# Retrieval stage of a two-block kernel: one fixed order for TensorE, ScalarE and GpSimd, filling blocks spread over each route, and low halves made by GpSimd in the first two routes

## Chip, cores and metric

One core of one Trainium2 chip runs the whole program in one launch. The metric is the device time of that launch in microseconds (us). The median of three runs of the kernel before is 3214.27 us (3212.13 to 3221.74). A difference of 0.3%, about 9.6 us, is about the least that a measurement of this kernel can tell from no change.

## What is computed

The reference applies two transformer-like blocks to 512 tokens of width 1024. The change lies in the retrieval part of the first block:

```python
def block(xb):                      # 128 tokens at a time
    q = (xb @ w_query).reshape(T, 8, 2, 128)
    s = einsum('thpk,hpnk->thpn', q, sub_keys)         # two score rows of 128 for each head
    top_s, top_i = top_k(s, 16)
    cand_s = top_s[:, :, 0, :, None] + top_s[:, :, 1, None, :]
    cand_i = top_i[:, :, 0, :, None] * 128 + top_i[:, :, 1, None, :]
    best_s, best_pos = top_k(cand_s, 16)               # 16 of 16384 experts for each head
    idx = take_along_axis(cand_i, best_pos)
    gate = softmax(best_s)
    act = gelu(einsum('td,thkd->thk', xb, expert_u[idx]))
    return einsum('thk,thkd->td', gate * act, expert_v[idx])
```

## The kernel before

Four token tiles of 128 are routed. The experts of tile 0 are fetched row by row with indirect DMAs (`sparse`). For tiles 1 to 3 (384 tokens) all 16384 experts are multiplied densely, in 128 blocks of 128 experts, and weighted by a matrix `Wd` that holds the gates where they belong and zero elsewhere.

A **filling block** is one of those 128 blocks of the first product. `usplit` makes it ready: ScalarE casts the loaded `raw` (512 KB) into its high half `whi`, and the engine in `lo_eng[0]` subtracts to get the low half `wlo`. Both halves are 128x1024. `ublock` runs 24 matmuls of 384 columns, 12 before its `yield` and 12 after, and ScalarE's Gelu (`ge`) ends it. Then SP writes the result to `gd` (192 KB). The first `AHEAD = 76` blocks are done in the retrieval stage, to keep TensorE at work while the tiles are routed. `lookahead(nb, ns, nd)` issues 2·nb half blocks, up to nd of the waiting `Wd` writes (256 KB each), and counts ns towards the next gathered row. At the first half of block b it also splits block b+1; there are three pairs of `whi` and `wlo`.

`route(t)` is VectorE's work: sums of candidates (`cs`, `ci`), top 16 for each of eight heads, and for each head a comparison, a product and a sum over 128x800 (`eq`, `ix`). ScalarE's one part in it is the exponential of the softmax. Every `yield` in it lets the caller issue a `lookahead(1, 0)`, one whole block. Its first `yield` stands after the first head's `ix`. For tiles 1 to 3 it ends with three transposes on TensorE, ScalarE's copy `pT`, and VectorE's `nT`.

`scatter(t)` builds `Wd` for a tile, four tokens at a time (32 times): VectorE makes `bo` and three `ao`, ScalarE makes the fourth `ao` (through `ab`), four matmuls write a PSUM tile, and ScalarE copies it to `stg`. The `ao` and `bo` of a step are made one step ahead. After every second step one half block is issued. At the end 32 writes of `stg` to `Wd` are put on the list `pend`.

The order in the program is: route 0 and 1, scatter 1, route 2, scatter 2, route 3, scatter 3, and a tail of whole blocks until 76 are done and `pend` is empty. That makes 19 blocks in the first two routes, 8 in each scatter, 11 in each later route and 11 in the tail. The framework's planner is free to order the instructions of each engine otherwise: among what it takes to be ready, the instruction that was written first goes first. `pin(engines)` takes that freedom away: it chains all instructions of the named engines that were written since `pos[0]`, in the order written. Before the change only the dense stage after the retrieval is pinned. SP's DMA queue runs in the planner's order throughout.

After the tail, the dense stage loads `Wd`, `gd` and `v` for each block (`load`, `mid`) and TensorE runs the second product (`down`).

Of the kernel before, what the change touches and what calls it, by code (L numbers as in the profile page):

```python
# [181 lines left out]
def build(tc, A, out):  # L182
    nc = tc.nc
    V, S, G, PE = nc.vector, nc.scalar, nc.gpsimd, nc.tensor
    with ExitStack() as ctx:
# [52 lines left out]
        def psum(tag="ps"):  # L238
            ps = banks[""].tile([128, T], F32, name=tag, bufs=banks[tag])
            return ps  # L240
# [24 lines left out]
        lo_eng = [G]  # L265
# [42 lines left out]
        def gemm_cm(*a, **k):  # L308
            for _ in gemm_gen(*a, **k):
                pass  # L310
# [148 lines left out]
        with rpool("hg") as hg:  # L459
# [15 lines left out]
            with rpool("hgl") as hl_:  # L475
# [38 lines left out]
                for l in range(9):  # L514
                    m = 1 << l
                    nb = 2 * T // (2 * m)
                    for g in range(2):
# [10 lines left out]
                        for hh in range(2):  # L528
                            h = 2 * g + hh
# [171 lines left out]
        pos = [0]  # L701

        def pin(engines):

            ins = nc.cur_bb.bb.instructions
            for n in range(pos[0], len(ins)):
                e = ins[n].engine
                if str(e).split(".")[-1] in engines:
                    if e in last:
                        tc.add_manual_dep(ins[n], last[e], mybir.DependencyInfo(  # L710
                            mybir.DependencyClass.NoSync, mybir.DependencyReason.DATA), reason="order")
                    last[e] = ins[n].name
            pos[0] = len(ins)
# [38 lines left out]
        with ExitStack() as rt0, ExitStack() as rt_:  # L752
# [51 lines left out]
                    nu[1] -= 1  # L804

            gemm_cm("w_q", range(16), 8, ah, al, cons_q, cols=128, late=LATE[1])

            lo_eng[0] = V
            rt_.close()
            rs = rt_.enter_context(rpool("rs"))  # L810

            def route(t):

                tf = rt.tile([128, 8, 2, 16], F32, name="tf")
                V.tensor_copy(tf.rearrange("p h a k -> p (h a) k"), ti[t])
                V.tensor_scalar(tf[:, :, 0], tf[:, :, 0], 128.0, None, op0=OP.mult)
                tv = ts[t].rearrange("p (h a) k -> p h a k", a=2)
                cs = rt.tile([128, 8, NCAND], F32, name="cs")
                ci = rt.tile([128, 8, NCAND], F32, name="ci")
                for src, dst in ((tv, cs), (tf, ci)):  # L820
                    for r in range(8):
                        V.tensor_add(dst[:, :, CO[r]:CO[r] + CN[r]], src[:, :, 0, r:r + 1].to_broadcast([128, 8, CN[r]]),
                                     src[:, :, 1, :CN[r]])
                    V.tensor_add(dst[:, :, CO[8]:], src[:, :, 0, 8:], src[:, :, 1, 0:1].to_broadcast([128, 8, 8]))
                bs = rt.tile([128, 8, 16], F32, name="bs")
                bp = rt.tile([128, 8, 16], U32, name="bp")
                for h in range(8):
                    V.max(bs[:, h, :8], cs[:, h])
                    V.max_index(bp[:, h, :8], bs[:, h, :8], cs[:, h])
                    c2 = rt.tile([128, NCAND], F32, name="c2", bufs=2)  # L830
                    V.match_replace(out=c2, in_to_replace=bs[:, h, :8], in_values=cs[:, h], imm_value=-3.0e38)
                    V.max(bs[:, h, 8:], c2)
                    V.max_index(bp[:, h, 8:], bs[:, h, 8:], c2)
                bpf = rt.tile([128, 8, 16], F32, name="bpf")
                V.tensor_copy(bpf, bp)
                pk = rt.tile([128, 3, 128], F32, name="pk")
                gt = pk[:, 0].rearrange("p (h k) -> p h k", h=8)
                V.tensor_sub(gt, bs, bs[:, :, 0:1].to_broadcast([128, 8, 16]))
                ix = rt.tile([128, 8, 16], F32, name="ix")
                for h in range(8):  # L840
                    eq = rt.tile([128, 16, NCAND], F32, name="eq", bufs=1)
                    V.tensor_tensor(eq, bpf[:, h, :, None].to_broadcast([128, 16, NCAND]),
                                    iota[:, None, :NCAND].to_broadcast([128, 16, NCAND]), op=OP.is_equal)
                    V.tensor_mul(eq, eq, ci[:, h, None, :].to_broadcast([128, 16, NCAND]))
                    V.reduce_sum(ix[:, h], eq, axis=AX.X)
                    if h == 2:
                        S.activation(gt, gt, AF.Exp)
                    if h == 4:
                        sm_ = rt.tile([128, 8], F32, name="sm_")
                        V.reduce_sum(sm_, gt, axis=AX.X)  # L850
                        V.reciprocal(sm_, sm_)
                        V.tensor_mul(gt, gt, sm_[:, :, None].to_broadcast([128, 8, 16]))
                    if h < 7:
                        yield
                if t == 0:
                    V.tensor_copy(idx0, ix.rearrange("p h k -> p (h k)"))
                    V.tensor_copy(gate0, pk[:, 0])
                    yield
                    return
                ii = rt.tile([128, 2, 128], I32, name="ii")  # L860
                V.tensor_copy(ii[:, 0], ix.rearrange("p h k -> p (h k)"))
                V.tensor_scalar(ii[:, 1], ii[:, 0], 127, None, op0=OP.bitwise_and)
                V.tensor_scalar(ii[:, 0], ii[:, 0], 7, None, op0=OP.logical_shift_right)
                V.tensor_copy(pk[:, 1:3], ii)
                for _ in range(3):
                    yield
                pp = psum()
                for a in range(3):
                    PE.transpose(pp[:, a * 128:(a + 1) * 128], pk[:, a], ident)
                pT = rt.tile([128, 3, 128], F32, name="pT", bufs=2)  # L870
                S.copy(pT.rearrange("p a t -> p (a t)"), pp[:, :384])
                nT = rt.tile([128, 2, 128], F32, name="nT", bufs=2)
                V.tensor_scalar(nT, pT[:, 0::2], -1.0, None, op0=OP.mult)
                tr[t] = pT, nT
                yield

            def scatter(t):

                pT, nT = tr[t]
                stg = rs.tile([128, 128, 128], F32, name="stg")  # L880

                def onehots(u):
                    bo = rs.tile([128, 4, 128], F32, name="bo", bufs=3)
                    V.tensor_tensor(bo, iota[:, None, :].to_broadcast([128, 4, 128]),
                                    pT[:, 1, u:u + 4, None].to_broadcast([128, 4, 128]), op=OP.is_equal)
                    aos = []
                    for w in range(4):
                        tk = u + w
                        ao = rs.tile([128, 128], F32, name="ao", bufs=8)
                        if w == 3:  # L890

                            ab = rt.tile([128, 128], F32, name="ab", bufs=2)
                            S.activation(ab, iota, AF.Abs, bias=nT[:, 1, tk:tk + 1])
                            S.activation(ao, ab, AF.Relu, scale=nT[:, 0, tk:tk + 1], bias=pT[:, 0, tk:tk + 1])
                        else:
                            V.tensor_scalar(ao, iota, pT[:, 2, tk:tk + 1], pT[:, 0, tk:tk + 1], op0=OP.is_equal, op1=OP.mult)
                        aos.append(ao)
                    return bo, aos

                oh = [onehots(0)]  # L900
                for u in range(0, 128, 4):
                    if u < 124:
                        oh.append(onehots(u + 4))
                    bo, aos = oh.pop(0)
                    pw = psum()
                    for w in range(4):
                        PE.matmul(pw[:, w * 128:(w + 1) * 128], aos[w], bo[:, w], start=True, stop=True)  # L907
                    S.copy(stg[:, :, u:u + 4].rearrange("p i t -> p t i"), pw.rearrange("p (t i) -> p t i", t=4))
                    if u % 8 == 4:
                        yield  # L910
                for i in range(0, 128, 4):
                    pend.append((Wd[i:i + 4, :, t * 128 - 128:t * 128].rearrange("i p t -> p i t"), stg[:, i:i + 4]))

            tr = {}
            for t in range(2):
                for _ in route(t):
                    lookahead(1, 0)
            for t in range(1, 4):
                nxt = route(t + 1) if t < 3 else iter(())
                for _ in scatter(t):  # L920
                    lookahead(.5, .25, 2)
                for _ in nxt:
                    lookahead(1, 0)


            while nu[0] < AHEAD or pend:
# [1275 lines left out]
```

## Time and profile before

| | us |
|---|---|
| median of three runs | 3214.27 |
| profiled execution | 3219.84 |
| its span, first to last instruction | 3218.1 |
| TensorE busy | 3078.4 (96%) |
| VectorE busy | 2157.9 (67%) |
| ScalarE busy | 1137.4 (35%) |
| GpSimd busy | 540.3 (17%) |

The span starts at 0. Busy times are shares of the whole span, over stages that have different limits. The mean granted clock of TensorE is 0.983 of full speed. In the chain of work that ended last TensorE has 74% and VectorE 8%.

### The profile page before, as it was taken

To read this page: it belongs to the slowest core of one execution; us is meant where nothing else is said; L and a number is where in the kernel's file an instruction comes from. 1 tells how busy PE (TensorE), PEld (TensorE's weight loads), DVE (VectorE), ACT (ScalarE), POOL (GpSimd) and SP (SyncE) were. 2 spreads that over 40 slices of the span, in tenths; PEclk is the share of its full clock that TensorE was granted. 3 is DMA by queue.
4 is the path that set the end of the run, shared out by engine and by line. 5 is a ranking of instruction groups with operands and counts; after the bars stand their busy time and mean duration, and the time that the engine had idled before them with its cause. 6 is when DMAs were issued, how large, how long until landed. Compare 5 with 4: busy or idle time off the path is not lost.

```text
span 3218.1 us, 53697 instructions
## 1 busy us (share of the span) xinstructions
PE 3078.4 (96%) x21497; PEld 2402.0 (75%) x21497; DVE 2157.9 (67%) x4369; ACT 1137.4 (35%) x1787; POOL 540.3 (17%) x372
## 2 busy tenths in 40 slices
PE   6999998999999999999989999999999998999997
PEld 4877788999988889999977777777777775444443
DVE  5834789997568888999967767676676753232223
ACT  3123334784733333333343323332365431111111
POOL 2221211001034445565400000000000001000000
PEclk9999999999999999999999999999999998999999
DMA  5153335658699999999821212222355365999995
GB/s 207 53 207 120 131 108 176 191 185 289 195 374 396 370 364 339 356 362 360 329 96 61 75 64 87 75 74 74 138 213 193 118 236 211 393 396 409 399 406 218
DMA packets 235855, 727.90 MB, mean 226 GB/s; under 512 B 22032, under 2 KB 110864, under 8 KB 198608
## 3 DMA queue, kind: packets, MB, share of 16 engines
q1 hardware_dynamic: 188464, 569.74, 47.8%
q0 software_dynamic: 36864, 134.23, 11.4%
q10 hardware_dynamic: 10272, 20.45, 1.7%
q8 instruction: 170, 2.79, 0.3%
q14 instruction: 85, 0.70, 0.1%
HBM read 661.03 MB, written 63.31 MB: 225 GB/s over the span
## 4 chain that ended last, share of the span: by engine, by line
PE 74%; DVE 8%; ACT 2%; DMA 2%; issue 1%; SPq 0%; POOL 0%; ACTq 0%; DVEq 0%
PE pg L695 12%; PE pf L1991 7%; PE pg L291 5%; PE pg L292 5%; PE pg L293 5%; PE py L1034 5%; PE py L1033 5%; PE py L1032 5%; PE pd L2026 3%; PE pg L1726 2%; PE ps L907 2%; PE pc L1372 1%; PE pc L2040 1%; DVE wlo L263 1%; PE pf L1319 1%; PE pt L2068 1%
## 5 line engine op out<-in xcount | busy, mean ns | idle before, releaser
L262 ACT CAST whi<-raw 128x1024 fp32r<-128x1024 f32 x294 | 307.6, 1048 | 697.8 <-PE pg L292 366.1
L263 DVE TENSOR_TENSOR wlo<-raw,whi 128x1024 fp32r<-128x1024 f32 x250 | 306.6, 1227 | 198.6 <-ACT whi L262 193.8
L291 PE MATMUL pg<-ah,whi 128*128 128x512 f32 x1056 | 427.8, 406 | 0.3 <-ACT whi L262 0.3
L293 PE MATMUL pg<-ah,wlo 128*128 128x512 f32 x1056 | 421.5, 400 | 3.0 <-POOL wlo L263 2.5
L292 PE MATMUL pg<-al,whi 128*128 128x512 f32 x1056 | 423.2, 401 | 0.0
L695 PE MATMUL pg<-ah,wlo 128*128 128x384 f32 x1024 | 346.3, 338 | 15.5 <-DVE wlo L263 15.5
L695 PE MATMUL pg<-ah,whi 128*128 128x384 f32 x1024 | 350.8, 343 | 6.1 <-ACT ge L697 5.5
L695 PE MATMUL pg<-al,whi 128*128 128x384 f32 x1024 | 346.0, 338 | 0.0
L725 POOL DMA_INDIRECT g<-in_u_dram,idx x128 | 196.9, 1538 | 626.0 <-DVE g L737 310.1
L1032 PE MATMUL py<-vh,gh 128*128 128x512 f32 x756 | 295.3, 391 | 3.0 <-ACT gh L262 2.6
L1033 PE MATMUL py<-vl,gh 128*128 128x512 f32 x756 | 295.7, 391 | 0.8 <-DVE vl L263 0.8
L1034 PE MATMUL py<-vh,gl 128*128 128x512 f32 x756 | 296.1, 392 | 0.0
L291 PEld LDWEIGHTS pg<-ah,whi 128*128 128x128 f32 x1056 | 200.3, 190 | 49.0 <-issue 6.9
L293 PEld LDWEIGHTS pg<-ah,wlo 128*128 128x128 f32 x1056 | 199.7, 189 | 48.0 <-POOL wlo L263 3.3
L292 PEld LDWEIGHTS pg<-al,whi 128*128 128x128 f32 x1056 | 200.0, 189 | 42.1 <-issue 3.6
L725 POOL DMA_INDIRECT g<-in_v_dram,idx x128 | 189.3, 1479 | 130.0 <-DVE y L745 95.8
L695 PEld LDWEIGHTS pg<-ah,wlo 128*128 128x128 f32 x1024 | 194.5, 190 | 16.8 <-DVE wlo L263 16.8
L695 PEld LDWEIGHTS pg<-ah,whi 128*128 128x128 f32 x1024 | 194.9, 190 | 9.5 <-ACT ge L697 6.5
L1991 PE MATMUL pf<-we,XT 128*64 128x512 f32 x720 | 197.6, 595 | 2.3 <-ACT XT L2077 2.3
L695 PEld LDWEIGHTS pg<-al,whi 128*128 128x128 f32 x1024 | 194.8, 190 | 2.5
L2043 DVE TENSOR_TENSOR mrg<-mrg,pc 128x512 f32<-128x512 f32 x128 | 84.5, 684 | 139.7 <-PE pc L2041 139.7
L1032 PEld LDWEIGHTS py<-vh,gh 128*128 128x128 f32 x756 | 142.3, 188 | 32.2 <-ACT gh L262 3.0
(680 smaller groups left out, 5783.2 us busy)
## 6 DMA issues: line engine op xcount, KB each, us to landing
raw<-in_uT_dram SPq DMA_DIRECT2D x128, 512.0 KB, 5.5
raw<-in_v_dram SPq DMA_DIRECT2D x128, 512.0 KB, 7.6
raw<-in_w_in_dram SPq DMA_DIRECT2D x54, 1024.0 KB, 4.9
we<-in_we_down_dram SPq DMA_DIRECT2D x47, 1024.0 KB, 9.5
we<-in_we_up_dram SPq DMA_DIRECT2D x46, 1024.0 KB, 9.8
we<-in_we_gate_dram SPq DMA_DIRECT2D x44, 1024.0 KB, 9.1
araw<-in_w_ada_dram SPq DMA_DIRECT2D x24, 1024.0 KB, 6.4
Wd<-stg SPq DMA_DIRECT2D x96, 256.0 KB, 5.2
```

What stands on the lines that cost most here:

```text
L262: S.copy(dst_hi, src)
L263: (eng or V).tensor_sub(dst_lo, src, dst_hi.bitcast(F32))
L291: a = PE.matmul(ps, l_ix(lh, k), r_ix(rh, k), start=k == 0, stop=False)
L292: a = PE.matmul(ps, l_ix(lh, k), r_ix(rl, k), start=False, stop=False)
L293: a = PE.matmul(ps, l_ix(ll, k), r_ix(rh, k), start=False, stop=k == kc - 1)
L695: PE.matmul(ps[:, :ND], w[:, k], a[:, k, 128:], start=k + n == 0, stop=k + n == 9)
L725: G.indirect_dma_start(out=raw, out_offset=None, in_=u if i < 128 else v, in_offset=bass.IndirectOffsetOnAxis(ap=idx0[:, k:k + 1], axis=0))
L1032: PE.matmul(py[t][d], gh[:, tk], vh[:, dsl], start=b == 0, stop=False)
L1033: PE.matmul(py[t][d], gh[:, tk], vl[:, dsl], start=False, stop=False)
L1034: PE.matmul(py[t][d], gl[:, tk], vh[:, dsl], start=False, stop=b == 127)
L1991: PE.matmul(pp[e * CAP:(e + 1) * CAP], xg(hf * 4 + k, e), ws[e][k], start=hf + k == 0, stop=hf == 1 and k == 3)
L2026: PE.matmul(pd[e * CAP:(e + 1) * CAP], hT[:, k, e * CAP:(e + 1) * CAP], ws[e][k], start=k == 0, stop=k == 3)
```

## The change

The three engines TensorE, ScalarE and GpSimd get the order of the program from route 0 to the end of scatter 3; VectorE and SP stay free. The low halves of the blocks issued in routes 0 and 1 are made by GpSimd instead of VectorE. The `yield`s of a route move: after `cs`, after `ci`, after heads 3 and 7 of the top 16, after five of the eight `ix`, and one instead of three ahead of the transposes. A scatter issues two half blocks after its first one-hot tiles and ahead of its first matmul. Block counts become 21 in the first two routes, 9 in each scatter, 11 in each later route and 6 in the tail.

```diff
             gemm_cm("w_q", range(16), 8, ah, al, cons_q, cols=128, late=LATE[1])
-
-            lo_eng[0] = V
             rt_.close()
...
                     V.tensor_add(dst[:, :, CO[8]:], src[:, :, 0, 8:], src[:, :, 1, 0:1].to_broadcast([128, 8, 8]))
+                    yield
...
                     V.max_index(bp[:, h, 8:], bs[:, h, 8:], c2)
+                    if h % 4 == 3:
+                        yield
...
-                    if h < 7:
+                    if h in (1, 3, 4, 5, 6):
                         yield
...
                 V.tensor_copy(pk[:, 1:3], ii)
-                for _ in range(3):
-                    yield
+                yield
                 pp = psum()
...
                 oh = [onehots(0)]
+                yield
+                yield
                 for u in range(0, 128, 4):
...
             tr = {}
+
+            pos[0] = len(nc.cur_bb.bb.instructions)
             for t in range(2):
                 for _ in route(t):
                     lookahead(1, 0)
+            pin(("PE", "Activation", "Pool"))
+            lo_eng[0] = V
             for t in range(1, 4):
                 nxt = route(t + 1) if t < 3 else iter(())
                 for _ in scatter(t):
                     lookahead(.5, .25, 2)
                 for _ in nxt:
                     lookahead(1, 0)
+                pin(("PE", "Activation", "Pool"))
```

## Rows read from the trace of the kernel before

**Rows 1.** Busy time by stretch: routes 0-1, scatter 1, route 3, tail.

```profile
core 0: us, PE busy (x) PEld busy (x) DVE busy (x) ACT busy (x) POOL busy (x), PEclk, DMA share, GB/s
452.20:552.60 100.40, 85.00 (x476) 83.32 (x475) 99.94 (x331) 36.19 (x47) 8.71 (x8) 0.93 0.54 177
552.60:613.00 60.40, 59.63 (x431) 58.79 (x430) 59.82 (x195) 59.90 (x111) 1.87 (x2) 1.00 0.31 100
...
728.00:786.30 58.30, 51.48 (x281) 50.67 (x279) 38.21 (x52) 18.53 (x28) 13.78 (x9) 0.94 1.05 352
...
849.80:897.60 47.80, 47.50 (x274) 47.18 (x272) 12.15 (x11) 15.99 (x23) 3.75 (x4) 1.00 1.03 323
```

**Rows 2.** Stretches, the filling blocks' matmuls (L695) alone: PE, PEld, PEclk, DMA.

```profile
452.20:552.60 100.40, 83.95 (x462) 82.09 (x463) 0.93 0.54 177
...
452.20:849.80 397.60, 293.09 (x1552) 274.06 (x1553) 0.96 0.58 191
```

**Rows 3.** Timeline of TensorE in scatter 1: start, length, line, tiles.

```profile
578.18 0.42 PE L695 MATMUL pg<-ah,whi 128*128 128x384 f32 x1
...
580.36 1.95 PE L907 MATMUL ps<-bo,ao 128*128 128x128 f32 x16
582.06 0.42 PE L695 MATMUL pg<-ah,whi 128*128 128x384 f32 x1
```

**Rows 4.** Timeline of TensorE after its longest waits; in brackets the wait.

```profile
508.12 0.69 PE L695 MATMUL pg<-ah,wlo 128*128 128x384 f32 x1 [11.75 <-DVE wlo L263]
...
762.97 0.69 PE L695 MATMUL pg<-ah,whi 128*128 128x384 f32 x1 [3.52 <-ACT ge L697]
...
768.58 0.37 PE L695 MATMUL pg<-ah,wlo 128*128 128x384 f32 x1
...
786.35 0.98 PE L907 MATMUL ps<-bo,ao 128*128 128x128 f32 x3 [3.35 <-DVE ao L896]
```

**Rows 5.** Timeline of GpSimd and of VectorE, 113 to 152 us.

```profile
113.30 5.10 POOL L263 TENSOR_TENSOR wlo<-raw,whi 128x1024 fp32r<-128x1024 f32 x1 [17.24 <-ACT whi L262]
...
149.19 2.38 POOL L263 TENSOR_TENSOR wlo<-raw,whi 128x1024 fp32r<-128x1024 f32 x1 [9.47 <-ACT whi L262]
...
149.28 2.84 DVE L523 TENSOR_TENSOR qP<-q,pre 128x512 f32<-128x512 f32 x1
152.04 0.68 DVE L524 TENSOR_TENSOR kS<-kk,suf 128x512 f32<-128x512 f32 x1
```

**Rows 6.** VectorE's groups by line, 452.2 to 550.8 us: count, busy, mean.

```profile
L263 DVE TENSOR_TENSOR wlo<-raw,whi 128x1024 fp32r<-128x1024 f32 x19 | 23.1, 1217 | 0.2 <-ACT whi L262 0.2
L842 DVE TENSOR_TENSOR eq<-bpf,cst 128x800 f32<-128x800 f32 x16 | 15.8, 986 | 0.0
...
L845 DVE TENSOR_REDUCE ix<-eq 128x16 f32<-128x800 f32 x16 | 15.7, 979 | 0.0
L737 DVE SCALAR_TENSOR_TENSOR g<-g,hT 128x1024 f32<-128x1024 f32 x4 | 4.9, 1219 | 0.0
```

**Rows 7.** Timeline of ScalarE in scatter 1.

```profile
584.05 0.72 ACT L893 ACTIVATE ab<-cst,nT 128x128 f32<-128x128 f32 x2
584.63 1.07 ACT L262 CAST whi<-raw 128x1024 fp32r<-128x1024 f32 x1
585.57 0.53 ACT L697 ACTIVATE ge<-pg 128x384 f32<-128x384 f32 x1
585.95 1.13 ACT L908 COPY stg<-ps 128x512 f32<-128x512 f32 x1
586.81 0.54 ACT L894 ACTIVATE ao<-ab,pT,nT 128x128 f32<-128x128 f32 x1
587.19 1.14 ACT L908 COPY stg<-ps 128x512 f32<-128x512 f32 x1
```

**Rows 8.** Timeline of SP's queue and of TensorE where the dense stage starts.

```profile
882.31 3.12 SPq L801 DMA_DIRECT2D Wd<-stg  x5
...
886.55 0.38 SPq L992 DMA_DIRECT2D raw<-Wd  x1
...
897.70 0.50 PE L1032 MATMUL py<-vh,gh 128*128 128x512 f32 x1 [0.41 <-ACT vh L262]
```

## Prediction

> **What bounds the kernel now.** I read the table of stretches first, because the change touches only one stage, 452 to 898 us. In its first two routes VectorE is busy for 99.94 of 100.40 us while TensorE has 85.00 [rows 1]: there VectorE sets the pace. In scatter 1 TensorE and ScalarE are both full (59.63 and 59.90 of 60.40 us). In route 3 and in the tail the DMA engines are full (shares 1.05 and 1.03), and VectorE and ScalarE are not. No single engine bounds the stage.
>
> Then I ask what the stage would take if TensorE never waited. In the tail it does nothing but filling blocks: 274 matmuls in 47.80 us, so 24 take 4.19 us, one block [rows 1]. In a scatter, half a block and two steps repeat every 582.06 − 578.18 = 3.88 us, of which the two steps are 1.70 and a slower first matmul some 0.09 [rows 3]; sixteen such pairs are 28.6 us for each scatter. Up to the end of scatter 3 TensorE ran 1552 / 24 = 64.7 blocks [rows 2], so its work there is 64.7 × 4.19 + 3 × 28.6 = 356.9 us, plus 2.2 (an estimate) for what is left of the query product. The stretch is 397.6 us: 38.5 us are lost. In the first two routes the same sum is 100.40 − 462 / 24 × 4.19 − 2.2 = 17.5 us lost [rows 1, 2].
>
> The timeline of TensorE says where. The longest wait, 11.75 us, is for a low half that stood behind a whole top-16 on VectorE; 3.52 us are a block whose load came late; 3.35 us are the start of scatter 3, waiting for VectorE's `ao` [rows 4], and scatter 2 starts with the same wait. After such a wait matmuls start 0.33 us apart instead of 0.175: from 762.97 to 768.58 us there are 17 of them, at the lower of the clock's two levels, which costs 2.6 us on top of the wait [rows 4].
>
> **The change, part by part.**
>
> *Low halves on GpSimd.* VectorE made 19 of them for 23.1 us [rows 6]. GpSimd needs 2.38 us for one when nothing disturbs it, 2.38 of a block's 4.19 us, so its own time fits. But the two engines disturb each other. Where both ran, VectorE's product of two tiles took 2.84 us instead of 0.68: it ended when GpSimd did, and 2.16 us were lost. The other way round GpSimd's subtraction took 5.10 us instead of 2.38, behind a run of such products [rows 5]. Routes are made of the same kind: the comparison and the product of 128x800 (0.99 us each) read two tiles. The sum after them (0.98 us) reads one [rows 6].
>
> No row shows these three beside GpSimd, so I bound the price of a low half: nothing at best, 2.16 us at worst, 2.16 − 0.98 = 1.2 us when it starts together with the sum. I take 1.7, between the last two, because the planner slips short one-tile operations between the long ones, where GpSimd gets in; and I take it for 16 of the 20 halves that fall ahead of route 1's transposes, since in the rest of a route (the top 16) VectorE reads one tile at a time. That is 27 us.
>
> The Trainium skill ("SBUF — State Buffer", section "SBUF: two separate sides") says that a VectorE instruction with two SBUF inputs and a GpSimd instruction that reads SBUF exclude each other, for the whole instruction of whichever started first. The rows above agree for 128x512 products; by the rule the 128x800 ones pay too, as I have it, and without it VectorE would be done at 520 us and the sum below would be some 12 us lower.
>
> *When the first two routes end.* VectorE's 99.94 us less 23.1 for low halves, less 4.9 for four gathered rows [rows 6], which now come later because GpSimd issues their gathers behind its last low half, less some 4 (an estimate) that already belong to route 2 and scatter 1, are 68 us. With 27 for the exclusion the transposes of route 1 come at 452.2 + 68 + 27 = 547 us. TensorE, in program order, has 20 blocks ahead of them: 452.2 + 2.2 + 83.8 = 538 us. It waits 9 us and pays 2.6 for the clock. Then come two blocks, and scatter 1 starts at 547 + 2.6 + 0.2 + 8.4 = 558 us with 22 blocks done, against 552.6 with 19.25: 2.75 blocks (11.5 us) more for 5.6 us, a gain of 5.9.
>
> *Two half blocks ahead of a scatter's first matmul.* They cover the chain from transposes to `ao`. The two waits of 3.35 us with their slow clock, 2 × 5.9 = 11.8 us, go. What cover hides: if VectorE is more than a block late there, the wait comes back.
>
> *ScalarE in program order.* Now `ge` of block b stands where it was written, right behind that block's second half, and everything behind it waits: the fourth `ao` of the next steps, on which the fourth matmul of a step depends, `stg`, and the next `whi`. The planner had put `ge` later, beside `whi` [rows 7]. From the end of a block: `ge` 0.38, `ab` and `ao` 0.67, `stg` 0.86, again 0.67 and 0.86, `whi` 0.94, then `ab` and the whole `ao` 0.83: 5.21, plus 0.2 for signals (an estimate), is 5.4 us. TensorE wants that `ao` after 3.88 + 0.85 + 0.64 = 5.37 us. So the stall is about nothing, or 0.37 us if every `ao` costs its full 0.54 instead of 0.38. Over 24 periods that is 0 to 9 us; I take 3. In the routes the same order leaves `ge`, `whi` and GpSimd's 2.38 us, some 3.9 us in a row, under a block's 4.19 plus the two matmuls that need no low half.
>
> *Five blocks more ahead of the tail.* Their loads (512 KB), `gd` writes (192 KB) and ScalarE work move with them, into stretches where DMA has room (share 0.31 in scatter 1 [rows 1]). The work moved is 5 × 4.19 = 21 us. Scatter 3 ended at 849.8; now at 849.8 + 21 − 5.9 − 11.8 + 3 = 856 us. The 3.52 us wait of route 3 I leave in: its DMA queue is as full as before.
>
> *The tail.* It gives back less than 21 us. SP issued the last `Wd` writes at 882 to 885, the first load of the dense stage at 886.55, and its first matmul came at 897.70, 11.2 us later [rows 8]. The 32 writes stay: 8.4 MB and six `gd` writes at the stretch's 323 GB/s [rows 1] are 30 us, against 25 us of TensorE's six blocks. I take the first load 27 us after scatter 3, and the dense stage 27 + 11.2 + 2.6 (clock) = 41 us after it, where it was 47.9: 7 us less.
>
> *Sum.* 6 us later at scatter 3, 7 us less in the tail: −1 us, 3219 us against the profiled 3219.84. That execution lies 5.6 us over the median, so the forecast is 3213 us beside 3214.27: no change that 0.3% (9.6 us) could show.
>
> **Rivals.** *Faster: GpSimd hardly holds VectorE up.* For it speaks that the planner can put one-tile work beside low halves; against it, that 48 operations of 128x800 fill half of these routes. Then TensorE's 20 blocks set the start (538), 9 + 2.6 us go, and the time is 3202 us; without the late load in route 3, 3198.
>
> *Faster: the tail does not bind,* and the dense stage follows the sixth block at once: 41 becomes 31 us, 3203 us. Against it: DMA share 1.03 there.
>
> *Slower: every low half shuts VectorE out in full.* 20 × 2.16 = 43 us instead of 27, scatter 1 starts 16 us later: 3229 us. For it speaks that the one full collision shown cost just that. It decides from 1.9 us for each of the 20 halves on.
>
> *Slower: ScalarE's order costs a scatter 0.6 us a period,* if all four matmuls wait for the fourth `ao`: 24 × 0.6 = 14 instead of 3 us, 3224 us; with one other small loss past the bound.
>
> **How the numbers follow.** The forecast has 0.44, with its own range of 3206 to 3222. GpSimd harmless 0.26, tail not binding 0.06, full exclusion 0.16, ScalarE's order 0.08. So faster 0.32, same 0.44, slower 0.24. Cutting a tenth on either side of the cases gives 3198 to 3230.
>
> **What would show it.** Low halves on GpSimd well above 2.38 us and `eq` operations above 2 us beside them; the transposes of route 1 near 547 us behind a TensorE wait for VectorE's `pk`; no 3 us wait at scatters 2 and 3; a scatter period near 7.9 us; scatter 3 done near 856 and the dense stage starting near 897. Wrong it would be if VectorE, still free in its order, put other work ahead of a low half in routes 2 and 3, or if the planner ordered later stages anew.

## The result: slower, 3246 us

The median of the changed kernel is 3246.18 us (3238.23 to 3248.43, four runs) against 3216.51 us of the kernel before: ratio 1.0092, 95% interval [1.0076, 1.0107]. The forecast was 3213 us, no change, with a range up to 3230. The profiled execution took 3245.69 us, with a span of 3243.9 us against 3218.1.

All of the span's 25.8 us are lost ahead of the dense stage, whose first matmul comes 26.7 us later, at 924.38 us instead of 897.70. From there to the end both kernels take 2320 us. The changed kernel's stage also began earlier: the query product ahead of it ended at 448.2 us, not 452.7 (it lies between 446.4 and 452.7 in all runs below; why was not looked into). Counted from there the stage is 31 us longer. The stretches are read first, as in [rows 1]: routes 0 and 1, route 2, route 3 and the tail of the kernel after.

```profile
core 0: us, PE busy (x) PEld busy (x) DVE busy (x) ACT busy (x) POOL busy (x), PEclk, DMA share, GB/s
454.20:568.50 114.30, 91.35 (x504) 89.03 (x502) 114.09 (x354) 35.51 (x50) 56.83 (x24) 0.91 0.50 148
637.50:704.20 66.70, 58.48 (x305) 54.93 (x304) 54.54 (x145) 22.96 (x32) 19.44 (x14) 0.95 1.04 348
768.70:821.20 52.50, 52.50 (x304) 52.20 (x304) 20.79 (x30) 22.53 (x32) 0.00 (x0) 1.00 1.01 319
886.30:924.40 38.10, 27.09 (x157) 26.77 (x155) 6.05 (x7) 10.10 (x15) 3.64 (x4) 0.91 1.04 325
```

Measured as in the prediction (a block is 24 x 0.1735 us, a scatter's own matmuls 28.6 us), TensorE loses 27.8 us ahead of scatter 1 (before some 19); 9.1 us in scatter 1 (before 1.6); 14.8 us in route 2 (before 3.9); 0.6 us in route 3 (before 10.4); 4.5 and 5.1 us in scatters 2 and 3 (before 3.3 and 3.0); and 11.2 us in the tail (before 0.7). The differences add up to the 31 us. The timeline of TensorE shows the single waits, in brackets, as in [rows 4]:

```profile
548.17 0.47 PE L869 MATMUL ps<-cst,pk 128*128 128x128 f32 x1 [11.59 <-DVE pk L853]
568.48 2.08 PE L909 MATMUL ps<-bo,ao 128*128 128x128 f32 x8 [6.95 <-DVE ao L896]
...
667.34 0.44 PE L695 MATMUL pg<-ah,wlo 128*128 128x384 f32 x1 [1.29 <-DVE wlo L263]
...
924.38 0.79 PE L1039 MATMUL py<-vh,gh 128*128 128x512 f32 x1 [11.02 <-ACT vh L262]
```

**At scatter 1.** The transposes of route 1 came at 548 to 550 us; the forecast had 547. But the two half blocks that were to cover the chain from there to `ao` ran out, and TensorE waited 6.95 us more. The timelines of VectorE and of ScalarE show why:

```profile
549.99 0.28 DVE L865 CAST pk<-ii 128x256 f32<-128x256 int32 x1
...
555.93 0.98 DVE L843 TENSOR_TENSOR eq<-bpf,cst 128x800 f32<-128x800 f32 x1
...
566.37 0.99 DVE L845 TENSOR_TENSOR eq<-eq,ci 128x800 f32<-128x800 f32 x1
567.27 0.29 DVE L873 TENSOR_SCALAR nT<-pT 128x256 f32<-128x256 f32 x1
...
568.08 0.85 DVE L896 TENSOR_SCALAR ao<-cst,pT 128x128 f32<-128x128 f32 x3
```

```profile
551.05 0.48 ACT L871 COPY pT<-ps 128x384 f32<-128x384 f32 x1 [13.89 <-PE ps L869]
...
567.60 0.40 ACT L893 ACTIVATE ab<-cst,nT 128x128 f32<-128x128 f32 x1 [9.68 <-DVE nT L873]
```

`pT` was ready at 551.5 us. VectorE, never idle, made `nT` at 567.27: in between it did what belongs to later routes (top 16, `tf`, `cs`, and four heads' `eq`).

**In route 2.** GpSimd issued 14 gathers of 512 KB here, 13 of them up to 688 us (first and last row of its timeline). In route 2 of the kernel before there were four, in its route 3 nine. ScalarE then waited for the blocks' own loads, five times and 15.8 us in all, and VectorE 12.2 us for ScalarE's `whi`; ScalarE's timeline shows the last three of such waits.

```profile
639.75 1.44 POOL L725 DMA_INDIRECT g<-in_u_dram,idx  x1 [46.53 <-DVE g L737]
...
693.70 1.35 POOL L725 DMA_INDIRECT g<-in_u_dram,idx  x1 [5.11 <-DVE nT L873]
```

```profile
689.08 1.05 ACT L262 CAST whi<-raw 128x1024 fp32r<-128x1024 f32 x1 [2.76 <-DMA raw<-in_uT_dram]
...
696.33 1.04 ACT L262 CAST whi<-raw 128x1024 fp32r<-128x1024 f32 x1 [5.44 <-DMA raw<-in_uT_dram]
...
702.24 1.05 ACT L262 CAST whi<-raw 128x1024 fp32r<-128x1024 f32 x1 [3.66 <-DMA raw<-in_uT_dram]
```

The views of the transfers in route 2 (637.5 to 704.2 us; in the kernel before, second, 613.3 to 664.9 us; q0 is GpSimd's queue, then packets, MB, share) add it up: 23.24 MB for 16.97. At the 348 GB/s of this stretch the 6.3 MB more are some 18 us (an estimate); the stretch is 15 us longer. Its blocks alone are 12.5 x 4.16 = 52 us of TensorE's time.

```profile
DMA packets 21948, 23.24 MB, mean 348 GB/s; under 512 B 1066, under 2 KB 18858, under 8 KB 21945
...
q0 software_dynamic: 2016, 7.34, 30.7%
```

```profile
DMA packets 20231, 16.97 MB, mean 329 GB/s; under 512 B 880, under 2 KB 18672, under 8 KB 20228
...
q0 software_dynamic: 450, 1.65, 11.5%
```

The DMA engines were full there before, too (share 1.02, in the kernel before's row of the stretch):

```profile
613.30:664.90 51.60, 48.28 (x279) 47.94 (x279) 51.60 (x146) 22.19 (x32) 5.19 (x4) 1.00 1.02 329
```

**In the tail.** After its sixth block TensorE waits 11.02 us for `vh`. The load behind it was issued at 917.73 us, behind the last `Wd` writes in SP's queue (compare [rows 8]), and the cast that makes `vh` waited for it until 923.29 (SP's queue, then ScalarE):

```profile
914.35 1.65 SPq L801 DMA_DIRECT2D Wd<-stg  x3
...
917.73 0.38 SPq L1012 DMA_DIRECT2D raw<-in_v_dram  x1
```

```profile
923.29 1.04 ACT L262 CAST vh<-raw 128x1024 fp32r<-128x1024 f32 x1 [2.85 <-DMA raw<-in_v_dram]
```

### The profile page after: what moved, and what is told of

Its sections match the earlier page's. It is cut to its first block, busy times and chain, and to the rows that moved or that the text cites. A ratio compares the mean times of both kernels' runs of the same rounds, so it can differ in the third digit from the quotient of the medians.

```text
span 3243.9 us, 53688 instructions
## 1 busy us (share of the span) xinstructions
PE 3086.3 (95%) x21497; PEld 2402.7 (74%) x21497; DVE 2162.8 (67%) x4347; ACT 1147.2 (35%) x1787; POOL 596.3 (18%) x394
## 3 DMA queue, kind: packets, MB, share of 16 engines
q0 software_dynamic: 36864, 134.23, 11.2%
## 4 chain that ended last, share of the span: by engine, by line
PE 77%; DVE 11%; ACT 6%; issue 2%; DMA 2%; SPq 0%; POOL 0%; ACTq 0%; DVEq 0%; POOLq 0%
PE pg L695 9%; PE pg L291 8%; PE pg L293 8%; PE pg L292 8%; PE pf L1998 7%; PE py L1041 5%; PE py L1040 5%; PE py L1039 5%; PE pd L2033 3%; PE pg L1733 3%; ACT stg L910 2%; PE pc L2047 1%; PE pc L1379 1%; PE pf L1326 1%; DVE eq L843 1%
## 5 line engine op out<-in xcount | busy, mean ns | idle before, releaser
L263 DVE TENSOR_TENSOR wlo<-raw,whi 128x1024 fp32r<-128x1024 f32 x228 | 279.9, 1228 | 212.3 <-ACT whi L262 211.1
L695 PE MATMUL pg<-ah,wlo 128*128 128x384 f32 x1024 | 347.3, 339 | 10.1 <-DVE wlo L263 7.3
L695 PE MATMUL pg<-ah,whi 128*128 128x384 f32 x1024 | 350.6, 342 | 4.3 <-ACT whi L262 3.7
L695 PE MATMUL pg<-al,whi 128*128 128x384 f32 x1024 | 345.3, 337 | 0.0
L263 POOL TENSOR_TENSOR wlo<-raw,whi 128x1024 fp32r<-128x1024 f32 x66 | 165.9, 2516 | 379.1 <-ACT whi L262 379.1
L695 PEld LDWEIGHTS pg<-ah,wlo 128*128 128x128 f32 x1024 | 194.2, 190 | 15.3 <-DVE wlo L263 11.0
L695 PEld LDWEIGHTS pg<-ah,whi 128*128 128x128 f32 x1024 | 194.5, 190 | 7.8 <-ACT whi L262 4.9
L695 PEld LDWEIGHTS pg<-al,whi 128*128 128x128 f32 x1024 | 194.5, 190 | 2.5
```

Of the source, the lines that this page charges most:

```text
L263: (eng or V).tensor_sub(dst_lo, src, dst_hi.bitcast(F32))
L695: PE.matmul(ps[:, :ND], w[:, k], a[:, k, 128:], start=k + n == 0, stop=k + n == 9)
```

## The experiments

The theory: what GpSimd and the fixed order cost by themselves was sized about right; what was missed is VectorE's own order, which stayed free. It put later routes ahead of scatter 1's first tiles, and gathered rows of later scatters, and with them their gathers, into route 2. Rivals: the exclusion itself; ScalarE's program order; the tail.

All runs in one table: the median, its ratio to the kernel before on the same chip with the 95% interval, and from the profiled execution scatter 1's first matmul, the length of route 2 (last matmul of scatter 1 to first of scatter 2), the end of scatter 3, and the first matmul of the dense stage, all in us.

| | median | ratio | scatter 1 | route 2 | scatter 3 ends | dense |
|---|---|---|---|---|---|---|
| before | 3216.5 | | 552.9 | 51.6 | 849.3 | 897.7 |
| after | 3246.2 | 1.0092 [1.0076, 1.0107] | 568.5 | 66.6 | 886.3 | 924.4 |
| e1_vector_lows | 3221.6 | 1.0018 [1.0008, 1.0028] | 558.4 | 54.1 | 860.4 | 898.2 |
| e2_scatter_first | 3233.9 | 1.0055 [1.0034, 1.0075] | 560.9 | 67.7 | 876.0 | 913.7 |
| e3_rows_later | 3250.7 | 1.0112 [1.0090, 1.0134] | 577.8 | 55.1 | 880.0 | 918.1 |
| e4_no_cover | 3243.1 | 1.0085 [1.0064, 1.0106] | 568.6 | 56.8 | 877.6 | 921.6 |
| e5_rows_in_scatter | 3221.0 | 1.0009 [0.9998, 1.0019] | 561.0 | 53.4 | 863.5 | 901.5 |
| e6_first_loads_early | 3250.6 | 1.0091 [1.0075, 1.0107] | 571.3 | 66.8 | 889.9 | 923.8 |
| e7_gpsimd_lows_alone | 3228.3 | 1.0030 [1.0019, 1.0041] | 567.6 | 50.5 | 860.0 | 907.8 |
| e8_vector_lows_mended | 3218.4 | 0.9997 [0.9987, 1.0006] | 557.0 | 52.9 | 857.7 | 891.6 |
| e9_pin_alone | 3222.4 | 1.0019 [1.0010, 1.0028] | 549.4 | 50.8 | 850.6 | 898.4 |
| e10_80_blocks_vector | 3214.9 | 1.0001 [0.9992, 1.0010] | 557.2 | 52.9 | 858.0 | 904.3 |
| e11_80_blocks_gpsimd | 3220.0 | 1.0015 [1.0006, 1.0024] | 558.2 | 53.4 | 861.0 | 907.8 |

**e1_vector_lows.** GpSimd's part undone, all else kept.

```diff
             pos[0] = len(nc.cur_bb.bb.instructions)
+            lo_eng[0] = V
             for t in range(2):
```

> The changed kernel, but VectorE makes the low halves of routes 0 and 1 again. Theory (order): the 25 us by which VectorE's operations were lengthened beside GpSimd go, and 21 low halves of 1.22 us (25.6 us) come, so VectorE's work is the same; only the order that the planner gives it changes. 3238 us (3230 to 3246), route 1's transposes within 6 us of 548, the dense stage still starting after a wait of some 10 us. Rival (the lengthened operations are the loss): 25 us less work for the stage's pacing engine, 3219 us, scatter 1 starting near 550.

Measured 3221.6 us. By its number the rival had it, by its mechanism it had not: VectorE's 19 low halves take 23.1 us here and its `eq` 984 ns, and yet route 1's last VectorE step (`pk`) ends at 547.4, where it ended at 550.3. What differs is what came after: `nT` at 549.20 instead of 567.27, and 7 gathers in route 2, 3.90 MB. VectorE's work was about the same and the planner's order of it another one; how strongly that would tell was underestimated by 16 us. So 25 of the 29.7 us go with this one edit, and as many with e5's, which leaves the low halves with GpSimd: neither GpSimd's part nor the rest of the change makes the loss alone.

**e2_scatter_first.** The whole change, and VectorE may not begin route t+1 before the first one-hot tiles of scatter t (`behind` adds that order to each VectorE instruction written since `n0`).

```diff
                 oh = [onehots(0)]
+                mark[0] = [x for x in nc.cur_bb.bb.instructions if str(x.engine).endswith("DVE")][-1].name
...
+                n0 = len(nc.cur_bb.bb.instructions)
                 for _ in nxt:
                     lookahead(1, 0)
+                behind(n0)
```

> The changed kernel, but every VectorE instruction of route 2 (and 3) stands behind the first one-hot tiles of scatter 1 (and 2). Theory (VectorE's order puts route 2 ahead of scatter 1): route 1's transposes come 6 us earlier, near 542, and scatter 1's first matmul near 553 instead of 568.5; VectorE's displaced work fits where it idled or multiplied gathered rows; 3232 us (3227 to 3238). Rival (VectorE's work is only moved): route 2 gets longer by what scatter 1 gains, 3246 us.

Measured 3233.9 us, 12.3 less than the whole change: near the theory's number, and not given back in route 2 (67.7 us against 66.6). `nT` follows `pT` at once, at 551.69 us. One thing was wrong: the transposes came at 549.5 us, not 542, so scatter 1 started at 560.9 and not 553. In part that is this execution's later start: its query product ended at 452.1 us, the changed kernel's at 448.2. Counted from there the transposes run from 97.3 to 98.6 us, against 99.9 to 102.4, so what VectorE had drawn ahead of them cost 2.6 to 3.8 us and not 6; and scatter 1 starts 11.4 us earlier, where the times in the table differ by 7.6.

**e3_rows_later.** No gathered row is counted in the scatters.

```diff
-                    lookahead(.5, .25, 2)
+                    lookahead(.5, 0, 2)
```

> The changed kernel, but no gathered row is counted in the three scatters; these rows come in the tail and the dense stage. Theory (13 gathers of 512 KB in route 2 delay the loads of its blocks): 6.8 MB at 348 GB/s are 19.6 us of that stretch's 66.7; route 2 loses some 5 us instead of 14.8 and the time is 3236 us (3231 to 3241). Rival (it is the order of VectorE and ScalarE there, not the transfers): 3246 us, with the same short waits for low halves in route 2.

In route 2 the theory held: 55.1 us, 3.2 lost instead of 14.8. But the time is 3250.7 us. The gathers were now written behind the part that is pinned, and the planner put them between GpSimd's low halves, where they wait for `idx0` of route 0. The timelines of GpSimd and of TensorE:

```profile
504.00 1.19 POOL L725 DMA_INDIRECT g<-in_u_dram,idx  x1 [13.21 <-DVE idx L857]
...
507.70 2.40 POOL L263 TENSOR_TENSOR wlo<-raw,whi 128x1024 fp32r<-128x1024 f32 x1
```

```profile
510.15 0.69 PE L695 MATMUL pg<-ah,wlo 128*128 128x384 f32 x1 [14.66 <-POOL wlo L263]
```

A second wait of 14.27 us follows at 566.58; the gather ahead of that low half had waited 15.99 us for VectorE's product of a row (`g`). And the dense stage, which now multiplies 13 rows more, is 10 us longer from its first matmul to its last (773.8 instead of 763.5 us).

**e4_no_cover.** The two `yield`s ahead of a scatter's first matmul removed; three blocks go to the tail.

```diff
                 oh = [onehots(0)]
-                yield
-                yield
```

> The changed kernel, but without the two half blocks ahead of each scatter's first matmul; three blocks go back to the tail. Theory (the cover is worth nothing here): scatter 1 still waits for VectorE's one-hot tiles, the 3.35 us waits of scatters 2 and 3 come back for two blocks of 4.2 us less, and the three blocks run in the tail in the 11 us in which TensorE waited: 3244 us (3238 to 3249). Rival (the cover saves what the prediction gave it): 11.8 us of waits and slow clock come back for 8.4 us, and the blocks lengthen the tail: 3255 us.

Measured 3243.1 us, the theory's number. The dense stage waits 4.35 us for `vh` instead of 11.02, since three more blocks fill the tail, and scatter 1 starts where it did. Scatter 2 starts after a wait of 2.29 us, which the cover had hidden.

**e5_rows_in_scatter.** As e2, and a row's product stands behind the first one-hot tiles of the scatter that counts it.

```diff
+                    n0 = len(nc.cur_bb.bb.instructions)
                     V.scalar_tensor_tensor(g, g, 1.0, hT0, op0=OP.mult, op1=OP.mult, accum_out=lg0[:, k:k + 1])
+                    behind(n0)
```

> As e2_scatter_first (VectorE's part of a later route stands behind a scatter's first one-hot tiles), and a gathered row counted in a scatter is multiplied no earlier than that scatter's first one-hot tiles, so that its gather can't be drawn into the route ahead of it. Theory (13 gathers bunched in route 2 delay the loads of its blocks): route 2 loses 3 to 5 us instead of 15.9 and the dense stage starts near 902 instead of 913.7: 3222 us (3217 to 3228). Rival (the order of ScalarE and VectorE in route 2 causes the waits): route 2 as in e2, 3234 us.

Measured 3221.0 us. Of 29.7 us, 25 are gone, with GpSimd's low halves, the pinned engines and all `yield`s still in place. Route 2 takes 53.4 us, ScalarE no longer waits for `raw` there, and this is its traffic (626.8 to 680.2 us), 17.07 MB for 23.24, next to none of it gathered:

```profile
DMA packets 20339, 17.07 MB, mean 320 GB/s; under 512 B 883, under 2 KB 18803, under 8 KB 20337
...
q0 software_dynamic: 4, 0.02, 0.1%
```

The edge moves more than transfers: with the gathers go VectorE's products of these rows, 13 of 1.2 us in e2's route 2, where TensorE also waited 4.55 us for VectorE's `pk`. How much of the 14.3 us between e2 and e5 is transfers and how much VectorE's time is not separated; in the changed kernel, where VectorE idled 12.2 us behind ScalarE's waits, the trace speaks for the transfers.

**e6_first_loads_early.** The dense stage's first loads are written into the tail.

```diff
             while nu[0] < AHEAD or pend:
-                lookahead(1, .5)
+                lookahead(1, .5, 6)
+                if nu[0] == AHEAD - 2 and 0 not in vpre:
+                    for b in range(2):
+                        vpre[b] = rawtile((1, D))[:, 0]
+                        nc.sync.dma_start(vpre[b], A["v"][b])
+                if nu[0] == AHEAD - 1 and 0 not in wpre:
+                    wpre[0] = rawtile((2, 512))[:, :, :ND]
+                    nc.sync.dma_start(wpre[0][:, 0], Wd[0])
+                    nc.sync.dma_start(wpre[0][:, 1], gd[0])
```

> The changed kernel, but the dense stage's loads of v for blocks 0 and 1, and of Wd and gd for block 0, are written inside the tail, and the tail puts up to 6 Wd writes behind a block instead of 4. Theory (TensorE's 11.0 us wait at the end of the tail is for loads that stand behind the last Wd write in SP's queue): the wait shrinks to some 3 us, 3238 us (3234 to 3242). Rival (the DMA engines are full, so that what is loaded earlier makes something else later): the wait moves to block 1 or to the tail's blocks, 3246 us.

The rival. TensorE's wait at the start of the dense stage shrinks from 11.02 to 6.77 us, now for `gh`, which needs `Wd`; and block 1 waits 3.49 us (timeline of TensorE):

```profile
923.80 0.80 PE L1053 MATMUL py<-vh,gh 128*128 128x512 f32 x1 [6.77 <-ACT gh L262]
...
938.14 0.50 PE L1053 MATMUL py<-vh,gh 128*128 128x512 f32 x1 [3.49 <-ACT gh L262]
```

From the end of scatter 3 to the last matmul of the dense stage (1692.2 us here, 1687.9 in the changed kernel) it is 802.3 us, there 801.6: what the first block gained, the second lost. That full DMA engines are the reason (share 1.04 in the tail) was expected, but no run shows it alone; from 930 us on it is TensorE that is full, busy for 717 of 720 us up to 1650 in the changed kernel. The median is 4 us above the changed kernel's, with the four runs of either overlapping (3245 to 3256 us against 3238 to 3248).

**e7_gpsimd_lows_alone.** The kernel before with GpSimd's low halves in routes 0 and 1, nothing pinned or moved.

```diff
-            lo_eng[0] = V
             rt_.close()
...
+            lo_eng[0] = V
             for t in range(1, 4):
```

> The kernel before with one part of the change: GpSimd makes the low halves of routes 0 and 1; no order is fixed, no yield moved. Theory (what hurts is what VectorE's order becomes and where the gathers fall, not the exclusion by itself, which costs VectorE about what the low halves did): scatter 1 starts within 8 us of 553; 3221 us (3214 to 3230). Rival (GpSimd's low halves are the whole loss): 3240 us or more.

Measured 3228.3 us, 9.5 above the kernel before and inside the expected range; but scatter 1 starts 15 us later, not within 8. TensorE waits 14.10 us at 518.87, for ScalarE's `ge`, which stood behind an exponential that waited 17.61 us for VectorE's `pk` (timelines of ScalarE and of TensorE):

```profile
516.71 0.31 ACT L845 ACTIVATE pk<-pk 128x128 f32<-128x128 f32 x1 [17.61 <-DVE pk L836]
```

```profile
518.87 0.69 PE L695 MATMUL pg<-ah,whi 128*128 128x384 f32 x1 [14.10 <-ACT ge L697]
```

On GpSimd a gather stood ahead of a low half here too, with a wait of 13.08 us for `idx`, but that ended 8 us earlier, at 508.81. The transposes came at 560.64, after another 13.15 us of waiting for `pk`: VectorE, busy for 106.3 of the 106.4 us up to there, sets the start of scatter 1. The changed kernel has no such wait in routes 0 and 1 ahead of its transposes.

**e8_vector_lows_mended.** e5 with VectorE's low halves and the early loads of e6; the diffs are those of e1, e2, e5 and e6.

> The changed kernel with VectorE's low halves in routes 0 and 1 (as e1), the two order edges of e5, and the early loads of e6. Theory: against e1 (3222) scatter 1 starts some 5 us earlier and the wait at the end of the tail shrinks by 8 us: 3208 us (3203 to 3214), faster than both kernels. Rival (each gain is taken back by the next stage): 3221 us.

Measured 3218.4 us: no faster than the kernel before. The dense stage starts 6 us earlier than there, but its last matmul comes at 1659.8 against 1662.1 us.

**e9_pin_alone.** The kernel before with the three `pin` lines alone.

> The kernel before with one part of the change: TensorE, ScalarE and GpSimd get the order of the program from route 0 to scatter 3; VectorE makes the low halves, the yields stand where they stood. Theory (the fixed order costs ScalarE's scatters little, as the prediction had it): the scatters lose 6 to 13 us together, against 5.5 before, and the dense stage starts within 5 us of 897.7: 3218 us (3210 to 3224). Rival (program order costs ScalarE 0.6 us in each of 24 periods, or TensorE the low halves that VectorE makes late): 3231 us.

Measured 3222.4 us. By the measure used above TensorE loses 21.4 us in the three scatters, 7.9 in the kernel before: 13.5 more, where the expectation had at most 7.5 more. It gets 9 back in route 3 (1.3 lost instead of 10.4).

**e10_80_blocks_vector** and **e11_80_blocks_gpsimd.** `AHEAD = 80` in e8 without its early loads, and in e5.

> As e8 (low halves on VectorE, two order edges) without its early loads, and 80 filling blocks ahead of the dense stage instead of 76. Theory (the tail is bound by its transfers, TensorE idles 11 us in it): four more blocks lengthen the tail by their transfers alone, 4 x 0.7 MB at 325 GB/s or 8.6 us, and shorten the dense stage by 4 x 4.19 = 16.8 us: 3210 us (3205 to 3216). Rival (what follows is no faster by them, or the tail grows by the whole blocks): 3218 us.

> As e5 (the whole change and the two order edges, low halves on GpSimd), with 80 filling blocks ahead of the dense stage instead of 76. Theory: 8 us less than e5's 3221: 3213 us (3207 to 3219). Rival: as e5, 3221 us.

Measured 3214.9 us, inside the theory's range, and 3220.0 us, where e5 had been, as the rival had it. The tail took 46.3 and 46.8 us, 8.3 and 8.8 more than in e5, as expected from its transfers, but what follows shrank less than by four whole blocks: from the end of scatter 3 to the dense stage's last matmul 798.1 and 798.7 us, against 802.8 in e5. The two kernels differ in the engine for the low halves alone: the 5 us between them are GpSimd's price once the order is mended. No kernel here is measurably faster than the kernel before.

## Why the prediction was wrong

- **GpSimd's price: right in its sum, by luck in part.** Means of VectorE's groups up to 548.4 us, beside [rows 6]:

```profile
L843 DVE TENSOR_TENSOR eq<-bpf,cst 128x800 f32<-128x800 f32 x16 | 26.1, 1632 | 0.0
L845 DVE TENSOR_TENSOR eq<-eq,ci 128x800 f32<-128x800 f32 x16 | 17.7, 1106 | 0.0
L846 DVE TENSOR_REDUCE ix<-eq 128x16 f32<-128x800 f32 x16 | 15.6, 972 | 0.0
...
L813 DVE CAST tf<-ti 128x256 f32<-128x256 uint32 x3 | 4.5, 1488 | 0.0
...
L858 DVE COPY gate<-pk 128x128 f32<-128x128 f32 x1 | 1.6, 1575 | 0.0
```

  Against the kernel before, the two `eq` groups take 12.3 us more (26.1 + 17.7 against 15.8 + 15.7), the 24 and 16 sums of candidates some 9 more (440 and 408 ns each against 196 and 199), the casts and the copy 5: about 26.5 us, where 27 were forecast. The sum of one tile is not longer. The Trainium skill ("SBUF — State Buffer", section "SBUF: two separate sides") has the two-input operations shut out; the rows agree.

  But the 27 were 16 halves at 1.7 us, paid by the operations of 128x800; those paid 12.3, and the rest came from sums and copies that were put at nothing. Of the signs named, low halves "well above 2.38 us" did not come (2.37 to 3.00 us, 2.55 on average), and 5 of 16 comparisons were above 2 us. A small misreading: in [rows 5] VectorE's product ended 0.55 us after GpSimd's, not with it; the 2.16 us stand. The transposes at 548 us, beside 547 forecast, are partly luck too: counted from the end of the query product they came 5 to 8 us later than forecast.

- **"Two half blocks ahead of a scatter's first matmul. They cover the chain from transposes to `ao`": the step that failed.** It named its own condition, VectorE no more than a block late there, and did not ask what VectorE, still free in its order, would be doing. It was 16 us late with `nT`. e2 shows it: with that order alone mended scatter 1 starts 7.6 us earlier (11.4 from the end of the query product) and takes 65.3 instead of 69.1 us. At scatters 2 and 3 the cover did work: no 3 us wait is left.

- **Route 2 was not in the sum: the second step that failed.** It was taken as it was, with four gathers in it. The text saw that GpSimd "issues their gathers behind its last low half" and took that for VectorE's gain only, without asking into which stretch they would fall next: one whose transfers were already full (DMA share 1.02 before). It lost 14.8 us instead of 3.9; e5 against e2, gathers and products together: 67.7 to 53.4 us. The closing warning, that VectorE might put other work ahead of a low half in routes 2 and 3, came near it, but had no term and no chance.

- **Route 3: better than forecast.** The 3.52 us that were "left in" went too; 0.6 us are lost instead of 10.4.

- **ScalarE in program order: a size.** The three scatters lose 15.5 us in e5 against 7.9 before: 7.6 instead of the 3 taken, within the 0 to 9 given.

- **The tail: right.** 38.1 us against the 41 forecast, bound by transfers as it said. Scatter 3 ended at 886 instead of 856; the tail could give none of it back.

With VectorE's order mended (e5) the dense stage starts at 901.5 us, where the forecast had 897. So the sum held to some 5 us but for the two terms that VectorE's order sets, though its parts missed both ways: 3 us more at scatter 1's start, 7.5 at scatter 3's end, 3 less in the tail. The two terms are some 23 us: 7.5 at the start of scatter 1 (11.4 from the end of the query product), 3.3 in it, 13.3 in route 2, less 1.1 in what follows. None of the rivals was this one. The parts do not add up either: e9's 6 us and e7's 9.5 make 15.5 of the whole's 29.7. The moved `yield`s were not run alone, but with the pins (e1) they cost 5 us, no more than the pins by themselves (e9); so the other 14 us come from GpSimd's low halves and the fixed order together. Why the planner orders VectorE's work so was not tried.

## What to carry to other kernels

Where some engines are pinned and one stays free, ask what the free one will put ahead of the next critical chain: fixing the others changes its order too. A part that makes transfers later moves them into another stretch; add up the bytes of the stretch where they land. And where an engine runs its instructions in order, one that waits long is paid for by the work behind it: in e3 a gather on GpSimd that waited 13.21 us for its index, in e7 an exponential on ScalarE that waited 17.61 us.

## What the runs showed that was not expected

Beside GpSimd's low halves VectorE's copies of a single tile were longer too: `tf` 1488 ns on average against 286 in the kernel before, `gate` 1575 against 217; the reduction over 128x800 was not (972 against 979). In the tail the loads that were issued earlier gained nothing: 801.6 and 802.8 us from scatter 3 to the dense stage's last matmul in two kernels whose dense stages began after waits of 11.0 and 10.9 us (after, e5), and 802.3 us in e6, where that wait was 6.8 us and the next block waited 3.5.
